# TensorE in program order through attention, with one unit behind each weight block, a scaled input in PSUM, and queries scaled before they are rotated

## The chip, the cores and the metric

The kernel runs on one core of a Trainium2 chip. The metric is the time of one execution on the device in microseconds (us), smaller is better; runs of one kernel on one chip lie within a few tenths of a per cent. The engines of the core work side by side, each in the order of its own instructions: TensorE (PE in the rows, PEld for its weight loads), VectorE (DVE), ScalarE (ACT), GpSimd (POOL), and SyncE (SP), which here only issues DMAs. SBUF and PSUM are the on-chip memories; TensorE writes into PSUM.

## What is computed

Two layers over T = 256 tokens of width D = 2048, with a context of 256 tokens that only layer 0 reads. Everything is fp32. Cut to what matters here:

```python
# layer 0
h  = rmsnorm(x, g0) * (1 + scale) + shift            # scale, shift, gate = silu(c) @ ada_w + ada_b
hc = rmsnorm(ctx, g0) * (1 + scale_c) + shift_c
k, v, q, za, glu, zb = split(h @ w_in)               # 2 KV heads, 8 query heads of 128
q  = rope(rmsnorm(q) * q_norm);  k = rope(rmsnorm(k) * k_norm)
kc, vc = split(hc @ w_in[:, :512])                   # context keys and values
s  = (q @ concat(k, kc).T) * 128 ** -0.5             # per head: 256 queries x 512 keys
attn = softmax(s) @ concat(v, vc)
conv = silu(layernorm(depthwise_conv31(a * sigmoid(b)) + dw_b))    # a, b = split(glu), 1024 channels
x  = x + gate * (concat(attn * silu(za), conv * silu(zb)) @ w_out0)
# layer 1: adaLN-RMSNorm, projection, spatial gating, output projection, gated residual; then a final RMSNorm
```

## The kernel before

**Products.** Each fp32 matrix is split into a high and a low part, and each product is three TensorE instructions: high by high, high by low, low by high (L386, L388, L389 for 128x256 outputs, L409 to L411 for the 128x512 outputs of the queries, L560 to L564 for keys and values). The weights come as jobs of 512 KB, one block each. A job has a load (a DMA on SP's queue into `raw`, a ring of ten buffers), a split (ACT copies `raw` to `whi`, L361; then DVE or GpSimd makes `wlo` = `raw` − `whi`, L364; GpSimd has the jobs 30 to 133), and its products. `whi` and `wlo` have four buffers each.

**Modulation jobs.** Between the weight jobs lie others ("A" jobs) that make the modulation of the gate of layer 0 and of layer 1. They load `traw` into the same ring, and DVE works on each in two instructions (L274, in PSUM operand `cbp`). They have no TensorE work.

**The scaled input.** `make_h` makes the operand h of layer 0 (`h0`, names `h` in the trace) and of the context (`hc`) four blocks of 128 columns at a time: DVE makes `ht` = x · scale · 1/rms (L453), ACT adds the shift and rounds to the high part (L456), DVE makes the low part from `ht` and the high part (L460). `ht` lies in SBUF.

**PSUM.** Eight banks of 128x512: three for `acc` (products, and every second score), one for the score `S`, one for the convolution, one for `cbp`, two for all else (tag "m").

**Attention.** Keys and queries are normalised per head (`head_rstd`, L720 to L724: squares `sqj` on ACT, a root, a reciprocal), rotated (`rope`, L709 to L714, queries on DVE, keys on GpSimd), and transposed on TensorE. For each of 16 pieces (key head, half of the queries, query head): a score (`attn_head`, L776), its maximum on DVE (L779, L780), exp on ACT (L782) with the query's norm as its scale, four transposes `ptp` of the result P (L796), and for each two pieces a product `O` with the values (L807). `AD` = 3 is the distance between a score and its transposes.

**Order.** The Python program lists the segments and the "side" work, attention and convolution steps, which it hands out behind weight jobs:

```python
for _ in range(math.ceil((PACEA if key == "attn" else PACE) * len(side[key]) / max(1, left))):
```

So the number of steps behind a weight job follows from the steps left and the jobs left (`PACEA` = 1.25). The final order of each engine is set by the scheduler of the language, which estimates when each instruction can start; inside a priority it moves instructions past each other. The segments of layer 0 are, in order: the conv's projections with keys and values (`body`); the first half of the queries (`qa`), four blocks of the gate `za`, and the second half (`qb`); the rest of `za`; the gate of the convolution; and the output projection.

Of the kernel before, what the change touches and what calls it, by code (L numbers as in the profile page):

```python
# [44 lines left out]
P2 = 4  # L45
# [40 lines left out]
def backbone_kernel(  # L86
# [146 lines left out]


# [135 lines left out]
    def w_rows(jobs, src, kbs, h, post):  # L370
# [3 lines left out]
        for n, (kq, kts) in enumerate(parts):  # L374
            def mmf(jb, kq=kq, n=n, kts=kts):
# [3 lines left out]
                for kt in kts:  # L379
                    hh, hl = h(kq * 4 + kt)  # L380
                    k = kt - kts[0]
                    for b in range(2):
# [3 lines left out]
                        nc.tensor.matmul(o, wh, hh, start=(n == 0 and kt == kts[0] and b == 0), stop=False,  # L386
                                         skip_group_check=True)
                        nc.tensor.matmul(o, wh, hl, start=False, stop=False, skip_group_check=True)  # L388
                        nc.tensor.matmul(o, wl, hh, start=False, stop=end, skip_group_check=True)  # L389
# [4 lines left out]
    def w_cols(jobs, src_f, kbs, hs, post):  # L394
# [3 lines left out]
        for n, (kp, kts) in enumerate(parts):  # L398
            def mmf(jb, kp=kp, n=n, kts=kts):
# [3 lines left out]
                for i, (h, ch) in enumerate(hs):  # L403
                    for k, kt in enumerate(kts):
# [4 lines left out]
                        nc.tensor.matmul(accs[i], hh[:, sl], jb.hi[:, k, :], start=s0, stop=False)  # L409
                        nc.tensor.matmul(accs[i], hh[:, sl], jb.lo[:, k, :], start=False, stop=False)  # L410
                        nc.tensor.matmul(accs[i], hl[:, sl], jb.hi[:, k, :], start=False, stop=s1)  # L411
# [130 lines left out]

    def kv_part(kqs):
# [3 lines left out]
        for cg in range(2):  # L547
            accs = {}
            for kq in kqs:
                def mmf(jb, cg=cg, kq=kq, accs=accs):  # L550
                    for i, h in enumerate((hx, hcx)):
                        if kq == kqs[0]:
                            accs[i] = bank("acc")
                        for k in range(4):
                            hh, hl = h(kq * 4 + k)
                            for c in range(2):
# [5 lines left out]
                                nc.tensor.matmul(o, hh[:, sl], jb.lo[:, k, :], start=False, stop=False,  # L562
                                                 skip_group_check=True)
# [140 lines left out]
    def rope(dst, src, nm, c, nh, eng, t1, t2):  # L704
# [487 lines left out]
```

## Time and profile before

| | |
|---|---|
| runs shown | median 926.71 us of 3 (925.51 to 928.1) |
| profiled execution | 926.46 us, span 924.7 us |
| granted TensorE clock, mean | 0.975 |
| busy: TensorE, DVE, ACT, POOL | 872.9, 659.6, 457.9, 258.6 us |
| DMA | 239.06 MB, mean 259 GB/s |

A row of the timeline has the start and the length in us, the engine, the line of the kernel, the operation, what is written and read (buffer numbers left out), shape and type, and a count; in brackets stands how long the engine was idle before it and whose end released it. A group's row has its busy time, the mean ns of one, and the idle time before its instructions. A stage's row has the stretch, its length, the busy time of each engine with the number of its instructions, the granted clock, the share of the DMA engines' time and the GB/s.

### The profile page before, as it was taken

To read this page: it belongs to the slowest core of one execution; us is meant where nothing else is said; L and a number is where in the kernel's file an instruction comes from. 1 tells how busy PE (TensorE), PEld (TensorE's weight loads), DVE (VectorE), ACT (ScalarE), POOL (GpSimd) and SP (SyncE) were. 2 spreads that over 40 slices of the span, in tenths; PEclk is the share of its full clock that TensorE was granted. 3 is DMA by queue.
4 is the path that set the end of the run, shared out by engine and by line. 5 is a ranking of instruction groups with operands and counts; after the bars stand their busy time and mean duration, and the time that the engine had idled before them with its cause. 6 is when DMAs were issued, how large, how long until landed. Compare 5 with 4: busy or idle time off the path is not lost.

```text
span 924.7 us, 17928 instructions
## 1 busy us (share of the span) xinstructions
PE 872.9 (94%) x7084; PEld 800.5 (87%) x7084; DVE 659.6 (71%) x1413; ACT 457.9 (50%) x648; POOL 258.6 (28%) x125
## 2 busy tenths in 40 slices
PE   5999999599998689999999899999999999999994
PEld 3798899599887578998999778998899999999994
DVE  2355684978887877895765299998988977554442
ACT  5643242347557668545544544455583544444441
POOL 0000023659875235686777520000000000000000
PEclk9999999799999899999999899999999999999998
DMA  9999999685776332678889579988887788755402
GB/s 355 406 389 352 363 338 365 252 286 173 233 247 217 121 114 91 205 249 298 312 311 342 175 277 410 409 312 304 311 281 225 250 282 281 218 185 174 137 1 91
DMA packets 66864, 239.06 MB, mean 259 GB/s; under 512 B 7502, under 2 KB 7768, under 8 KB 66268
## 3 DMA queue, kind: packets, MB, share of 16 engines
q1 hardware_dynamic: 66780, 237.92, 72.9%
q8 instruction: 55, 0.90, 0.4%
q14 instruction: 29, 0.24, 0.1%
HBM read 235.80 MB, written 2.10 MB: 257 GB/s over the span
## 4 chain that ended last, share of the span: by engine, by line
PE 76%; DVE 10%; DMA 10%; ACT 3%; issue 1%; POOL 0%; SPq 0%; DVEq 0%; POOLq 0%; ACTq 0%
PE acc L386 17%; PE acc L389 16%; PE acc L388 16%; DMA traw<-adat 7%; PE acc L409 4%; PE acc L410 4%; PE acc L411 4%; DVE traw L274 4%; PE ada L317 3%; PE acc L560 2%; PE acc L562 2%; PE acc L564 2%; DVE conv L626 1%; DMA braw<-ada 1%; PE rms L191 1%
## 5 line engine op out<-in xcount | busy, mean ns | idle before, releaser
L361 ACT ACTIVATE whi<-raw 128x1024 fp32r<-128x1024 f32 (+1 forms) x256 | 263.4, 1031 | 285.1 <-PE acc L388 140.4
L364 POOL TENSOR_TENSOR wlo<-raw,whi 128x1024 fp32r<-128x1024 f32 x104 | 250.9, 2425 | 283.3 <-ACT whi L361 145.4
L364 DVE TENSOR_TENSOR wlo<-raw,whi 128x1024 fp32r<-128x1024 f32 (+1 forms) x152 | 176.8, 1165 | 83.3 <-ACT whi L361 81.7
L274 DVE SCALAR_TENSOR_TENSOR traw<-traw,cbp 128x512 f32<-128x512 f32 x256 | 165.3, 682 | 56.0 <-DMA traw<-adat 52.7
L386 PE MATMUL acc<-h,whi 128*128 128x256 f32 x512 | 152.4, 299 | 8.0 <-DVE gaT L532 6.7
L388 PE MATMUL acc<-h,whi 128*128 128x256 f32 x512 | 149.3, 293 | 0.4 <-DVE h L460 0.4
L389 PE MATMUL acc<-h,wlo 128*128 128x256 f32 x512 | 148.0, 290 | 1.6 <-POOL wlo L364 1.6
L388 PE MATMUL acc<-h1l,whi 128*128 128x256 f32 x512 | 145.2, 284 | 0.0
L389 PE MATMUL acc<-h1h,wlo 128*128 128x256 f32 x512 | 145.0, 283 | 0.0
L386 PE MATMUL acc<-h1h,whi 128*128 128x256 f32 x512 | 145.0, 283 | 0.0
L626 DVE SCALAR_TENSOR_TENSOR conv<-gaT,small,conv 128x241 f32<-128x241 f32 (+14 forms) x240 | 114.6, 478 | 5.2
L386 PEld LDWEIGHTS acc<-h,whi 128*128 128x128 f32 x512 | 100.6, 197 | 14.1 <-issue 10.3
L389 PEld LDWEIGHTS acc<-h,wlo 128*128 128x128 f32 x512 | 100.5, 197 | 4.1 <-issue 2.0
L388 PEld LDWEIGHTS acc<-h,whi 128*128 128x128 f32 x512 | 100.7, 197 | 3.5 <-issue 2.6
L388 PEld LDWEIGHTS acc<-h1l,whi 128*128 128x128 f32 x512 | 98.2, 192 | 0.1
L386 PEld LDWEIGHTS acc<-h1h,whi 128*128 128x128 f32 x512 | 98.2, 192 | 0.1
L389 PEld LDWEIGHTS acc<-h1h,wlo 128*128 128x128 f32 x512 | 98.2, 192 | 0.0
L389 PE MATMUL acc<-m1h,wlo 128*128 128x256 f32 x256 | 73.1, 286 | 0.0
L386 PE MATMUL acc<-m1h,whi 128*128 128x256 f32 x256 | 72.4, 283 | 0.0
L388 PE MATMUL acc<-m1l,whi 128*128 128x256 f32 x256 | 72.4, 283 | 0.0
L389 PEld LDWEIGHTS acc<-m1h,wlo 128*128 128x128 f32 x256 | 49.1, 192 | 2.9 <-issue 2.9
L411 PE MATMUL acc<-whi,h1l 128*128 128x512 f32 x128 | 51.1, 400 | 0.0
(235 smaller groups left out, 1649.1 us busy)
## 6 DMA issues: line engine op xcount, KB each, us to landing
traw<-adat SPq DMA_DIRECT2D x128, 512.0 KB, 5.0
raw<-w_out SPq DMA_DIRECT2D x64, 512.0 KB, 4.0
raw<-w_uz SPq DMA_DIRECT2D x64, 512.0 KB, 4.9
araw<-ada SPq DMA_DIRECT2D x56, 512.0 KB, 6.9
raw<-w_gate SPq DMA_DIRECT2D x56, 512.0 KB, 5.1
raw<-w_v SPq DMA_DIRECT2D x32, 512.0 KB, 5.1
raw<-w_q SPq DMA_DIRECT2D x16, 512.0 KB, 4.1
raw<-w_gate SPq DMA_DIRECT2D x16, 256.0 KB, 11.0
```

The lines of the kernel that those rows point to most:

```text
L274: nc.vector.scalar_tensor_tensor(out=jb.raw[:, k, :], in0=jb.raw[:, k, :], scalar=1.0, in1=cbq["t"], op0=ALU.mult, op1=ALU.mult, accum_out ...
L317: nc.tensor.matmul(st8["p"][32 * g : 32 * g + 32, :w], ccol[:, kb, :], jb.raw[:, a, q * w : (q + 1) * w], start=kb < 4 // nq, stop=kb >= N ...
L361: nc.scalar.activation(hv, jb.raw, AF.Copy)
L364: eng.tensor_tensor(out=jb.lo.rearrange("p a b -> p (a b)"), in0=jb.raw, in1=hv.bitcast(F32), op=ALU.subtract)
L386: nc.tensor.matmul(o, wh, hh, start=(n == 0 and kt == kts[0] and b == 0), stop=False, skip_group_check=True)
L388: nc.tensor.matmul(o, wh, hl, start=False, stop=False, skip_group_check=True)
L389: nc.tensor.matmul(o, wl, hh, start=False, stop=end, skip_group_check=True)
L409: nc.tensor.matmul(accs[i], hh[:, sl], jb.hi[:, k, :], start=s0, stop=False)
L410: nc.tensor.matmul(accs[i], hh[:, sl], jb.lo[:, k, :], start=False, stop=False)
L411: nc.tensor.matmul(accs[i], hl[:, sl], jb.hi[:, k, :], start=False, stop=s1)
L560: nc.tensor.matmul(o, hh[:, sl], jb.hi[:, k, :], start=kq == kqs[0] and k == 0 and c == 0, stop=False, skip_group_check=True)
L626: nc.vector.scalar_tensor_tensor(out=o, in0=y, scalar=w, in1=o, op0=ALU.mult, op1=ALU.add)
```

## The change

Five things change.

1. TensorE's instructions are held in program order from the first half of the queries to the start of layer 1: each is issued after the one before it in the program. Before, the scheduler was free to move them.
2. One attention step is now one `unit`: a score, the transposes of the piece three units back, and, every second time, a product with the values. One stands behind each weight block. The turns (transposes) of keys and queries are steps of their own; behind the second half of the queries two blocks have no step (`rest`). Attention steps and the query's rope run at high priority.
3. In `make_h`, `ht` of layer 0 and the context lies in a PSUM bank (tag "m").
4. `rope` works in place on its input, with two temporaries in SBUF; for queries the input is the product's PSUM bank.
5. Queries are scaled by their norm before the rotation (four ACT instructions of 128x128 for each 128 tokens and half), so that the score needs no scale: the maximum is taken negated in one DVE instruction, and L780 is gone. `P2`, which had no effect (`nw % 4 < 4`), goes.

```diff
+    pe = {"on": False}
+    def inorder(op, *args, **kw):
+        with tc.issue_after(pe["last"]) if pe["on"] and "last" in pe else nullcontext():
+            i = op(*args, **kw)
+        pe["last"] = i.ins
+    def matmul(*args, **kw):
+        inorder(nc.tensor.matmul, *args, **kw)
...
-            t = tmp.tile([128, 2, T], F32, tag="t2", name="ht", bufs=TB)
+            if m == 4:
+                t = bank("ht").rearrange("p (a b) -> p a b", a=2)
+            else:
+                t = tmp.tile([128, 2, T], F32, tag="t2", name="ht", bufs=TB)
...
-    def rope(dst, src, nm, c, nh, eng, t1, t2):
+    def rope(dst, src, nm, c, nh, eng):
         e, o = src[:, :, 0:64], src[:, :, 64:128]
-        eng.tensor_tensor(out=t1, in0=e, in1=tb(0), op=ALU.mult)
+        eng.tensor_tensor(out=t1, in0=e, in1=tb(2), op=ALU.mult)
+        eng.tensor_tensor(out=e, in0=e, in1=tb(0), op=ALU.mult)
         eng.tensor_tensor(out=t2, in0=o, in1=tb(1), op=ALU.mult)
-        eng.tensor_tensor(out=dst[:, :, 0:64], in0=t1, in1=t2, op=ALU.subtract)
-        eng.tensor_tensor(out=t1, in0=e, in1=tb(2), op=ALU.mult)
-        eng.tensor_tensor(out=t2, in0=o, in1=tb(3), op=ALU.mult)
-        eng.tensor_tensor(out=dst[:, :, 64:128], in0=t1, in1=t2, op=ALU.add)
+        eng.tensor_tensor(out=o, in0=o, in1=tb(3), op=ALU.mult)
+        eng.tensor_tensor(out=dst[:, :, 0:64], in0=e, in1=t2, op=ALU.subtract)
+        eng.tensor_tensor(out=dst[:, :, 64:128], in0=o, in1=t1, op=ALU.add)
...
-        at["rq"][i, cg] = head_rstd(src, 4, "qss", HD ** -0.5)
+        r = head_rstd(src, 4, "qss", HD ** -0.5)
+        for h in range(4):
+            nc.scalar.activation(src[:, h * 128 : (h + 1) * 128], src[:, h * 128 : (h + 1) * 128], AF.Copy, scale=r[:, h : h + 1])
...
-        nc.vector.tensor_reduce(out=mx[:, 0:1], in_=S, axis=AX.X, op=ALU.max)
-        nc.vector.tensor_scalar(out=mx[:, 1:2], in0=mx[:, 0:1], scalar1=rq, scalar2=-1.0, op0=ALU.mult, op1=ALU.mult)
+        nc.vector.tensor_reduce(out=mx[:, 1:2], in_=S, axis=AX.X, op=ALU.max, negate=True)
-        nc.scalar.activation(P, S, AF.Exp, bias=mx[:, 1:2], scale=rq, accum_out=mx[:, 2:3])
+        nc.scalar.activation(P, S, AF.Exp, bias=mx[:, 1:2], accum_out=mx[:, 2:3])
...
+        def unit(n):
+            if n < len(todo):
+                attn_head(*todo[n])
+            if n > AD and (n - AD) % 2 == 0:
+                attn_pv(*todo[n - AD - 1])
+            if AD <= n < len(todo) + AD:
+                attn_tr(*todo[n - AD])
...
-    segs = [body, qa + kv[0] + za[:4] + qb, kv[1] + za[4:] + [za_ready], ...
+    segs = [body, [pe on] + qa + za[:2] + kv[0] + za[2:4] + qb + [rest = 2], za[4:8] + kv[1] + za[8:] + [za_ready], ...
```

The lines move by ten or more: L276 to L287 stand for L274 before, L377 for L364, L469 and L476 for L453 and L460, L548 for L532, L786 for L782; all wrapped TensorE instructions have L238. How the order of the instructions moves, at three places. The numbers behind the names are those of the buffers and differ between the two kernels.

The first place is DVE's order around the block of keys and values before the queries. `gaT` and `gbT` add up the products of `acc` and so free the banks that TensorE needs; `h0` and `hc` are the low parts of the input. Before:

```order
L532 TENSOR_TENSOR kv_sb_820<-acc_2139,kv_sb_820 128x2x256
L460 SCALAR_TENSOR_TENSOR h0_2267<-ht_2268,modv0_133,h0_2267 128x256
L274 SCALAR_TENSOR_TENSOR traw_2073,adat_139<-traw_2073,cbp_2219 128x512 x2
L460 SCALAR_TENSOR_TENSOR h0_2267<-ht_2268,modv0_133,h0_2267 128x256
L460 SCALAR_TENSOR_TENSOR h0_2267<-ht_2275,modv0_133,h0_2267 128x256 x2
L460 SCALAR_TENSOR_TENSOR hc_2491<-ht_2492,modc_135,hc_2491 128x256
L532 TENSOR_TENSOR gaT_136<-acc_2179,gaT_136 128x512
```

And after:

```order
L287 SCALAR_TENSOR_TENSOR traw_2063,adat_139<-traw_2063,cbp_2219 128x512
L548 TENSOR_TENSOR gaT_136<-acc_2179,gaT_136 128x512
L287 SCALAR_TENSOR_TENSOR traw_2063,adat_139<-traw_2063,cbp_2219 128x512
L476 SCALAR_TENSOR_TENSOR h0_2267<-ht_2268,modv0_133,h0_2267 128x256 x2
L476 SCALAR_TENSOR_TENSOR h0_2267<-ht_2275,modv0_133,h0_2267 128x256 x2
L287 SCALAR_TENSOR_TENSOR traw_2073,adat_139<-traw_2073,cbp_2219 128x512 x2
L287 SCALAR_TENSOR_TENSOR traw_2089,adat_139<-traw_2089,cbp_2219 128x512 x2
L469 SCALAR_TENSOR_TENSOR ht_2492<-cT1_325,modc_135,rBc_613 128x256
L548 TENSOR_TENSOR gbT_137<-acc_2225,gbT_137 128x512
```

`gaT` now stands ahead of all four `h0` of that group and of `hc`; the `ht` of the context comes later, and `gbT` behind its first.

The second place is TensorE's order in the score products (`S`, or `acc` for the score that takes a product's bank). Before, behind the second half of the queries, among the blocks of `za`:

```order
L776 MATMUL S_3411<-kT_2564,qT_3072 128x512
...
L776 MATMUL acc_3678<-kT_2564,qT_3072 128x512
L776 MATMUL S_3500<-kT_2564,qT_3072 128x512
L776 MATMUL S_3623<-kT_2564,qT_3072 128x512
L386 MATMUL acc_3801<-h0_316,whi_3644 128x256
```

And after, inside the second half of the queries:

```order
L238 MATMUL S_3358<-kT_2564,qT_3060 128x512
L238 MATMUL acc_3280<-whi_3276,h0_1090 128x512
...
L238 MATMUL S_3388<-kT_2564,qT_3060 128x512
L238 MATMUL acc_3280<-whi_3312,h0_1655 128x512
...
L238 MATMUL S_3423<-kT_2564,qT_3060 128x512
L238 MATMUL ptp_3432<-ident_86,P_3332 128x128 x4
```

Three scores in a row became one score behind the twelve products of each block; seven of the sixteen stand inside the second half of the queries, where two stood before.

The third place is what stands between these scores on DVE, and ahead of an exp on ACT. DVE after, between the maxima of two scores (`traw` is a modulation job, L633 the convolution):

```order
L784 TENSOR_REDUCE mx_3360<-S_3358 128x1
L633 SCALAR_TENSOR_TENSOR conv_2950<-gaT_136,small_84,conv_2950 128x250
L633 SCALAR_TENSOR_TENSOR conv_2950<-gaT_136,small_84,conv_2950 128x249
L287 SCALAR_TENSOR_TENSOR traw_3522,adat_140<-traw_3522,cbp_2991 128x512 x2
L787 RECIPROCAL mx_3360<-mx_3360 128x1
L633 SCALAR_TENSOR_TENSOR conv_2950<-gaT_136,small_84,conv_2950 128x248
L266 COPY cbp_3991<-cb_105 128x512
L784 TENSOR_REDUCE mx_3390<-S_3388 128x1
```

A pair of `traw` stands between two maxima, and its instruction needs the transfer of its job. ACT after, behind the second half of the queries (`whi` are splits of weight jobs, the scalings have `acc` in and out):

```order
L222 ACTIVATE qss_3565<-qss_3565,epsc_97 128x4
L766 ACTIVATE acc_3280<-acc_3280,qss_3540 128x128 x2
L374 ACTIVATE whi_3649<-raw_3409 128x1024
L766 ACTIVATE acc_3281<-acc_3281,qss_3565 128x128 x4
L374 ACTIVATE whi_3683<-raw_3478 128x1024
L374 ACTIVATE whi_3741<-raw_3608 128x1024
L786 ACT_TABLE_LOAD
L786 ACTIVATE P_3594,mx_3592<-S_3590,mx_3592 128x512
```

The exp of the last score of that half now stands behind the scalings and three splits.

More of the change, by code (lines that the diff above doesn't have):

```diff
@@ L44 @@
 L1 = 2
-P2 = 4
 NF = 3
@@ L385, in mmf @@
                         end = n == len(parts) - 1 and kt == kts[-1]
-                        nc.tensor.matmul(o, wh, hh, start=(n == 0 and kt == kts[0] and b == 0), stop=False,
+                        matmul(o, wh, hh, start=(n == 0 and kt == kts[0] and b == 0), stop=False,
                                          skip_group_check=True)
-                        nc.tensor.matmul(o, wh, hl, start=False, stop=False, skip_group_check=True)
-                        nc.tensor.matmul(o, wl, hh, start=False, stop=end, skip_group_check=True)
+                        matmul(o, wh, hl, start=False, stop=False, skip_group_check=True)
+                        matmul(o, wl, hh, start=False, stop=end, skip_group_check=True)
                 if n == len(parts) - 1:
@@ L582, in post @@
             def post(i, a, cg=cg):
-                rope_q(i, cg, a)
-                side["attn"].append(lambda: turn_q(i, cg))
+                with tc.high_priority():
+                    rope_q(i, cg, a)
             w_cols(js, lambda kp, cg=cg: w_q[cg, kp], range(16), [(hx, 0), (hx, 1)], post)
@@ L738, in rope_k @@
         if i < 2:
-            t1 = tmp.tile([128, 2, 64], F32, tag="rp1", name="rp1", bufs=1)
-            t2 = tmp.tile([128, 2, 64], F32, tag="rp2", name="rp2", bufs=1)
-            rope(kr, s3, "k", i, 2, nc.gpsimd, t1, t2)
+            rope(kr, s3, "k", i, 2, nc.gpsimd)
         else:
@@ L828, in attn_steps, with both @@
     def attn_steps():
-        out, half = [], 0
+        def both(f, *args):
+            return lambda: [f(i, *args) for i in range(2)]
+        out = [both(turn_k), lambda: [turn_k(i) for i in (2, 3)], both(turn_q, 0)]
         todo = [(kvh, c, hq) for kvh in range(NKV) for c in range(2) for hq in range(4)]
-        for n in range(len(todo) + AD):
-            if n == len(todo) // 2:
-                half = len(out)
-            if n < len(todo):
-                out.append(lambda n=n: attn_head(*todo[n]))
-            if n >= AD:
-                out.append(lambda n=n: attn_tr(*todo[n - AD]))
-                if (n - AD) % 2 == 1:
-                    out.append(lambda n=n: attn_pv(*todo[n - AD]))
-        out.append(("za", attn_gate))
-        out += [lambda: attn_fin(0), lambda: attn_fin(1)]
-        return out[:half], out[half:]
+        def unit(n):
[5 more added lines that the diff above has]
+                attn_tr(*todo[n - AD])
+        for n in range(len(todo) + AD + 1):
+            if n == len(todo) // 2:
+                out.append(("q", both(turn_q, 1)))
+            out.append(lambda n=n: unit(n))
+        return out + [("za", attn_gate), lambda: attn_fin(0), lambda: attn_fin(1)]
     def hm(kb):
@@ L1024, in drain @@
             s = side[key].pop(0)
-            (s[1] if isinstance(s, tuple) else s)()
+            with tc.high_priority() if key == "attn" else nullcontext():
+                (s[1] if isinstance(s, tuple) else s)()
             k += 1
@@ L1065, in backbone_kernel @@
     ada1b = adat_pair(1, 1024, D + 1024)
-    plan += [hook(lambda: prep1(0)), hook(sgu_const)]
+    plan += [hook(lambda: pe.__setitem__("on", False)), hook(lambda: prep1(0)), hook(sgu_const)]
     first = v_part(0) + u_part(0)
@@ L1074, in backbone_kernel @@
         if j.kind == "W":
-            j.pool = P0 <= nw < P1 and nw % 4 < P2
+            j.pool = P0 <= nw < P1
             nw += 1
@@ L1107, in backbone_kernel @@
             for key in ("attn", "conv"):
+                if key == "attn" and st.get("rest"):
+                    st["rest"] -= 1
+                    continue
                 ahead = [n for k, n in deadline.items() if k == key and n > p]
@@ L1110, in backbone_kernel @@
                 for _ in range(math.ceil((PACEA if key == "attn" else PACE) * len(side[key]) / max(1, left))):
-                    if side[key] and isinstance(side[key][0], tuple) and side[key][0][0] == "za" and "za" not in st:
+                    if side[key] and isinstance(side[key][0], tuple) and side[key][0][0] not in st:
                         break
```

48 lines of the change are left out of this document (20 added, 28 removed).

## The prediction

> **What bounds the kernel now.** I read the page first, then a table of the span by stage, then the waits of TensorE (PE) in the stretch that the change touches, and last the rows around the longest waits.
>
> ```profile
> span 924.7 us, 17928 instructions
> PE 872.9 (94%) x7084; PEld 800.5 (87%) x7084; DVE 659.6 (71%) x1413; ACT 457.9 (50%) x648; POOL 258.6 (28%) x125
> PE 76%; DVE 10%; DMA 10%; ACT 3%; issue 1%; POOL 0%; SPq 0%; DVEq 0%; POOLq 0%; ACTq 0%
> ```
>
> TensorE is busy 94% of the span and carries 76% of the chain that ended last. The change takes no product away, so it can only win time in which TensorE stands still or runs at a low clock: 924.7 − 872.9 = 51.8 us of idle time at most. The table by stage (stretch, its length, then busy time of PE, weight load, DVE, ACT, POOL with counts, granted clock, DMA share, GB/s) shows where it lies.
>
> ```profile
> 100.00:150.00 50.00, 50.00 (x626) 45.55 (x628) 31.43 (x59) 13.88 (x20) 8.29 (x3) 1.00 0.93 345
> 150.00:183.00 33.00, 23.65 (x212) 22.51 (x200) 29.33 (x54) 11.77 (x18) 19.55 (x8) 0.89 0.83 323
> 183.00:252.00 69.00, 68.81 (x466) 64.94 (x467) 55.95 (x135) 38.53 (x79) 52.43 (x34) 0.96 0.69 225
> 252.00:300.00 48.00, 45.43 (x251) 37.95 (x250) 39.49 (x103) 31.67 (x54) 32.57 (x14) 0.96 0.68 231
> 300.00:340.00 40.00, 30.35 (x166) 23.24 (x164) 31.91 (x83) 24.49 (x36) 14.62 (x7) 0.87 0.39 125
> 340.00:380.00 40.00, 40.00 (x286) 36.51 (x285) 34.49 (x90) 29.36 (x48) 18.09 (x8) 1.00 0.36 112
> 430.00:480.00 50.00, 49.45 (x405) 47.54 (x404) 34.38 (x92) 27.17 (x37) 38.24 (x16) 1.00 0.86 309
> ```
>
> Two stretches have room: 150 to 183 (9.4 us idle) and 252 to 340 (2.6 + 9.7 = 12.3 us idle, at a clock of 0.87 in the second half). From 340 on TensorE is full. In both the change moves something.
>
> **The first stretch, and what scaled input in PSUM does to it.** These rows stand around the idle time before 183 us.
>
> ```profile
> 156.30 2.39 POOL L364 TENSOR_TENSOR wlo<-raw,whi 128x1024 fp32r<-128x1024 f32 x1 [1.83 <-PE acc L562]
> 157.16 0.69 DVE L532 TENSOR_TENSOR kv_sb<-acc,kv_sb 128x512 f32<-128x512 f32 x1
> 161.40 2.40 POOL L364 TENSOR_TENSOR wlo<-raw,whi 128x1024 fp32r<-128x1024 f32 x1 [2.71 <-ACT whi L361]
> 161.45 2.38 DVE L344 SCALAR_TENSOR_TENSOR modc<-modc,small 128x4 f32<-128x4 f32 x1
> 164.97 1.66 DVE L453 SCALAR_TENSOR_TENSOR ht<-xT,modv,rB 128x256 f32<-128x256 f32 x4
> 169.81 12.35 POOL L364 TENSOR_TENSOR wlo<-raw,whi 128x1024 fp32r<-128x1024 f32 x5 [6.00 <-ACT whi L361]
> 172.22 0.58 PE L389 MATMUL acc<-h,wlo 128*128 128x256 f32 x1 [1.57 <-POOL wlo L364]
> 173.59 6.38 DVE L460 SCALAR_TENSOR_TENSOR h<-ht,modv,h 128x256 fp32r<-128x256 f32 x3
> 179.89 2.56 DVE L460 SCALAR_TENSOR_TENSOR hc<-ht,modc,hc 128x256 fp32r<-128x256 f32 x1
> 182.37 0.68 DVE L532 TENSOR_TENSOR gaT<-acc,gaT 128x512 f32<-128x512 f32 x1
> 183.19 0.55 PE L386 MATMUL acc<-h,whi 128*128 128x256 f32 x1 [6.68 <-DVE gaT L532]
> 184.18 1.27 DVE L460 SCALAR_TENSOR_TENSOR hc<-ht,modc,hc 128x256 fp32r<-128x256 f32 x3
> ```
>
> While GpSimd runs `wlo`, a DVE instruction with two SBUF tensors as input takes as long as the `wlo` that it meets: `modc` needs 2.38 us for 4 columns, `h` 6.38 us for three and `hc` 2.56 us for one, where three `hc` take 1.27 us with GpSimd idle. An instruction with one input in PSUM isn't held: `kv_sb` took 0.69 us in the middle of a `wlo`. In the order of DVE, `gaT` stands behind the held instructions, and it frees the bank that TensorE needs: 6.68 us.
>
> The change puts `ht` into PSUM. `h` and `hc` (L476 now) then have one SBUF input, so their four held instructions fall from 6.38 + 2.56 = 8.9 us to 4 x 0.42 = 1.7. The instruction that makes `ht` (L469) still reads two SBUF tensors, `xT` and `rB`. In the trace none of them met a `wlo` (1.66 us for four), so its price when it does is bounded by 0.42 us and, from `modc`, 2.4 us; I take 2.4 for each that meets one. I walked the new order with these durations. ACT now does `whi_2007` after the first two `h0`, so GpSimd's `wlo` before the gap starts at 164.9 instead of 161.4; TensorE waits for it 1.3 us longer at about 166. `wlo_2110` starts at 169.8 as before, TensorE goes on at 172.2 as before, and has 24 products of that block ahead, which at the pitch of the slow clock end at about 176.8. It then needs `gbT` of the block before, which stands behind one `ht`; that meets `wlo_2208` until 177.0, ends at 177.5, and `gbT` ends at 178.2. So TensorE goes on at about 178.3 instead of 183.19: a gain of 4.9 us; the 1.3 us are in it, since they only shorten the later wait. If no `ht` is held it goes on at 176.8, a gain of 6.4; if five more `ht` are held (5 x 2.4 us), the stretch gets 7 us longer. I take −5, between −6.4 and +7.
>
> The Trainium skill, SBUF — State Buffer, section "SBUF: two separate sides", says that DVE and GpSimd take a shared port pair as an exclusive lock for a whole instruction, a DVE instruction with two SBUF inputs among them. By that rule each `ht` that meets a `wlo` is held to its end, which no row here shows for `ht`; the rows of `h`, `hc`, `modc` and `kv_sb` (2.5, 2.56, 2.38 and 0.69 us) agree with it.
>
> **The second stretch: attention.** TensorE's waits there, and the rows that end them:
>
> ```profile
> 290.29 2.24 PE L807 MATMUL O<-PT,kv_sb 128*128 128x256 f32 x7 [2.57 <-ACT PT L797]
> 303.27 1.13 PE L776 MATMUL S<-kT,qT 128*128 128x512 f32 x2 [1.67 <-ACT P L782]
> 308.45 2.03 PE L776 MATMUL acc<-kT,qT 128*128 128x512 f32 x2 [2.99 <-ACT z0T L601]
> 314.65 1.41 PE L776 MATMUL S<-kT,qT 128*128 128x512 f32 x2 [2.25 <-ACT P L782]
> 335.29 1.57 PE L776 MATMUL S<-kT,qT 128*128 128x512 f32 x2 [2.59 <-ACT qT L770]
> ```
>
> They sum to 12.1 us. They come of bunching: score products `S` stand two and three in a row, and the second waits for max and exp of the first, since the bank `S` is one. The change lays one unit (one S, the transposes of an older P, every second time a P·V) behind each weight block, in fixed order, so 12 products of a block lie between two `S`. What one unit costs, by rows:
>
> ```profile
> 258.21 0.39 PE L411 MATMUL acc<-whi,h 128*128 128x512 f32 x1
> 258.44 0.40 PE L409 MATMUL acc<-whi,h 128*128 128x512 f32 x1
> L779 DVE TENSOR_REDUCE mx<-S 128x1 f32<-128x512 f32 x11 | 7.5, 686 | 4.0 <-PE S L776 3.9
> 313.72 0.78 ACT L782 ACTIVATE P<-S,mx,qss 128x512 f32<-128x512 f32 x1 [1.45 <-DVE mx L780]
> L780 DVE TENSOR_SCALAR mx<-mx,qss 128x1 f32<-128x1 f32 x16 | 3.1, 204 | 0.0
> 306.51 1.28 ACT L601 ACT_TABLE_LOAD   x1
> 283.80 1.04 ACT L361 ACTIVATE whi<-raw 128x1024 fp32r<-128x1024 f32 x1
> 284.75 0.26 ACT L720 ACTIVATE sqj<-acc 128x128 f32<-128x128 f32 x1
> 262.10 4.43 DMA traw<-adat
> 268.31 4.41 DMA traw<-adat
> 274.57 4.52 DMA traw<-adat
> 279.18 0.69 DVE L274 SCALAR_TENSOR_TENSOR traw<-traw,cbp 128x512 f32<-128x512 f32 x1 [1.06 <-DMA traw<-adat]
> ```
>
> Twelve products at 0.23 us are 2.75 us between two `S`. Max (0.69) and exp (0.78) take 1.5 us, so a unit passes without a wait if its max isn't late. What makes it late is the modulation work of layer 1 on DVE, pairs of `traw` instructions (2 x 0.69), each pair behind a transfer that lands 4.4 us after the pair before it has freed its buffer. Four such pairs stand between the units of the second half of the queries, each ahead of a max. So a pair comes every 6.2 us (262.10, 268.31, 274.57), and a unit lasts 2.75 + 0.9 for S + 0.4 for transposes, some 4 us. The pairs that matter end, by the walk, at 265.2, 271.0, 276.8 and 282.6; behind each come one to three small conv instructions (0.42 each), a max and an exp, so that the bank `S` is free at 268.8, 274.0, 279.7 and 284.2. TensorE would want it at 269.2, 272.8, 277.6 and 283.7 (each is the start of the `S` before, with its wait, plus the unit): the first unit has slack, and the next three wait 1.2, 2.1 and 0.5 us.
>
> The other new waits, each from the order: at the start of the second query half TensorE needs a bank that `z0T` reads, which stands in ACT behind a `whi` (1.04) and a table load (1.28): 1.04 + 1.28 + 0.6 less 1.4 us of products and 0.4 of transposes, 1.2 us. Behind the last block of that half, exp of `P_3594` stands in ACT behind eight `sqj` (0.26 and more each), the root with its table load, eight scalings, four `whi` and another table load. The last of these `whi` waits for a product that ends 0.2 us before TensorE wants the next `S`, so TensorE waits 1.04 + 1.28 + 0.78 = 3.1 us. In all 1.2 + 3.8 + 3.1 = 8.1 us of new waits against 12.1 that go: −4.0. The slower clock behind a wait costs both sides; 40 us at 0.87 with 30.35 busy is at most 0.13 x 30.35 = 3.9 us before, and two thirds of that for two thirds of the waits, −1.3. Sum for attention −5; its ends are −12 (all new waits vanish) and +8 (next part).
>
> **Edits at nothing.** The 16 scalings of the queries are new on ACT; the row nearest is `sqj`, 0.26 us, so 4.2 us, all in the two stretches behind a query half, where I counted them. The 16 `mx` instructions of L780 that go (3.1 us on DVE) are 0.2 us per unit on a chain that has slack. Rope in place has the same six operations with an input in PSUM; its bank is held some 1 us longer, and TensorE gets there later than that. Dropping P2 changes no job. Between 340 and 380 the DMA share is 0.36, so an earlier start of the output projection can load ahead; between 430 and 480 it is 0.86 at 309 GB/s, and since every transfer waits for a buffer that TensorE's progress frees, the whole plan shifts with TensorE.
>
> **The sum.** −5 −5 = −10. The profiled execution took 926.46 us (span 924.7), the median of the runs is 926.71, so 0.25 apart; I predict 916.6. A change under 0.3% (2.8 us) can't be told from none in this kernel.
>
> **Rivals.**
> Both stretches win (forecast), 912 to 921: chance 0.45.
> Only the first wins: the waits in attention are replaced in kind, −5, 921.5 to 923. For it: the new waits are as long as the old ones, and the order is held, so nothing fills them. Chance 0.18.
> All attention waits go, since a `traw` lands sooner when the rings run ahead: −5 −12 = 909 to 911. For it: in 252 to 300 the DMA share is only 0.68. Against: the pairs come 6.2 us apart in that very stretch. Chance 0.15.
> Slower: the transfers of `traw` set the pace of the units. If the max of each of the seven units in that half stands behind a pair, a unit takes 6.2 instead of 4 us: 7 x 2.2 = 15.4 new, and 4.3 for the two others, against 12.1 that go, +7.6, and nothing from the first stretch: 934; with the first stretch's gain 929. It decides from the point where more than five of the seven wait so. Against it: the order has four pairs there, not seven. Chance 0.12.
> No change: the `ht` instructions are held in place of `h` and `hc`, so that the first stretch wins nothing, and attention trades like for like: 924 to 928. Five more held `ht` at 2.4 us undo the first gain and what attention wins. Chance 0.10. The rule of the Trainium skill named above (SBUF — State Buffer, "SBUF: two separate sides") would have it so wherever an `ht` meets a `wlo`.
>
> The likeliest range is 912 to 921; so that the other cases are in, 907 to 927. Faster: 0.45 + 0.18 + 0.15 = 0.78; same 0.10; slower 0.12.
>
> **What would show it.** First stretch right: no `h` or `hc` of L476 over 0.6 us before 190 us, and the wait for `gaT` or `gbT` under 3 us; wrong: `ht` of L469 with 2.4 us each. Attention right: `S` strictly one per block, waits of 0.5 to 2.1 us put down to P, with a `traw` ahead of the max, and one of about 3 us behind the second query half; the waits for z0T and for two S in a row gone. The prediction is wrong if the waits in the units are over 2.5 us each, if the block matmuls wait for a rope (bank held), or if TensorE idles after 400 us where it didn't.

## The result, and the profile after

The changed kernel takes 916.9 us (median, 914.78 to 919.12, 4 runs), the kernel before 927.4 on the same chip: a ratio of 0.9884, 95% interval 0.9857 to 0.9911. The forecast was 916.6, of 907 to 927. The sum is right; of its parts, the one for attention is too small, and a loss behind attention was missed, as shown below. Profiled executions of kernels that hardly differ up to 210 us end keys and values anywhere between 200.9 and 206.4 us (table below), so a difference of a few microseconds between two single profiles shows nothing alone.

The page of the profile after: the span, each engine's busy time, and the chain that ended last.

```profile
span 913.0 us, 17916 instructions
PE 867.9 (95%) x7084; PEld 799.7 (88%) x7084; DVE 649.8 (71%) x1397; ACT 457.6 (50%) x662; POOL 257.5 (28%) x125
PE 79%; DMA 9%; DVE 7%; ACT 2%; issue 1%; POOL 1%; SPq 0%; DVEq 0%; POOLq 0%; ACTq 0%
```

DVE's share of the chain fell from 10 to 7%. By stage (columns as in the prediction):

```profile
150.00:183.00 33.00, 29.43 (x282) 27.76 (x274) 26.76 (x64) 13.18 (x20) 18.32 (x8) 1.00 0.98 389
252.00:300.00 48.00, 42.55 (x218) 33.41 (x218) 41.64 (x114) 36.79 (x75) 29.74 (x13) 1.00 0.66 212
300.00:340.00 40.00, 39.46 (x263) 34.42 (x264) 34.62 (x82) 28.55 (x46) 18.00 (x8) 0.96 0.44 139
430.00:480.00 50.00, 47.82 (x380) 46.33 (x379) 36.35 (x93) 24.10 (x31) 36.41 (x16) 0.97 0.90 324
```

The stretch 150 to 183 is busy for 29.4 us instead of 23.7, and 300 to 340 for 39.5 instead of 30.4, at a clock of 0.96 instead of 0.87. From 430 to 480, TensorE idles 2.2 us where it idled 0.6. These stretches are cut by time, and the work in them has moved.

Three rows of TensorE's timeline in each kernel cut the span at the same work: the last product of keys and values, the first of the output projection (`mAh`), and the first of layer 1. Before, then after:

```profile
211.64 0.28 PE L564 MATMUL acc<-whi,hc 128*128 128x256 f32 x1
416.62 0.28 PE L386 MATMUL acc<-mAh,whi 128*128 128x256 f32 x1
529.33 0.80 PE L409 MATMUL acc<-whi,h1h 128*128 128x512 f32 x1
```

```profile
205.85 0.28 PE L238 MATMUL acc<-whi,hc 128*128 128x256 f32 x1
401.40 0.28 PE L238 MATMUL acc<-mAh,whi 128*128 128x256 f32 x1
516.02 0.80 PE L238 MATMUL acc<-whi,h1h 128*128 128x512 f32 x1
```

The gain is 5.8 us at the end of keys and values, 15.2 at the output projection, 13.3 at layer 1, and 11.7 in the span. So in this pair of profiles the first stretch gave 5.8, attention 9.4, and 3.5 were given back after it. The stages between these cuts hold the same products (attention, output projection, layer 1; before, then after; a count that differs by one is a record missing from a trace):

```profile
211.92:416.62 204.70, 192.48 (x1241) 170.08 (x1240) 174.29 (x432) 126.66 (x205) 130.00 (x65) 0.97 0.57 186
416.62:529.33 112.71, 107.26 (x861) 99.10 (x859) 62.02 (x164) 55.34 (x73) 79.66 (x34) 0.99 0.82 289
529.33:924.70 395.37, 383.51 (x2805) 361.04 (x2804) 294.76 (x533) 190.02 (x227) 4.77 (x2) 0.98 0.70 244
```

```profile
206.13:401.40 195.27, 187.56 (x1241) 167.22 (x1240) 167.58 (x410) 126.78 (x216) 130.60 (x67) 0.99 0.62 196
401.40:516.02 114.62, 109.44 (x860) 101.11 (x859) 64.40 (x169) 55.09 (x73) 79.78 (x34) 0.97 0.82 285
516.02:913.00 396.98, 385.37 (x2805) 362.32 (x2804) 295.35 (x533) 190.05 (x227) 4.77 (x2) 0.98 0.71 242
```

Attention's 9.4 us are 4.5 us less idle time of TensorE (7.7 instead of 12.2) and 4.9 us less busy time for the same products, at a clock of 0.99 instead of 0.97. The same cuts for every kernel that ran, from its profiled execution, with the timed ratio to the kernel before (95% interval):

| kernel | keys/values end | to first mAh | to layer 1 | ratio |
|---|---|---|---|---|
| before | 211.9 | 204.7 | 112.7 | 1 |
| changed | 206.1 | 195.3 | 114.6 | 0.9884 (0.9857 to 0.9911) |
| e1 changed, ht in SBUF | 213.4 | 196.8 | 117.1 | 0.9956 (0.9932 to 0.9981) |
| e2 before, ht in PSUM | 203.4 | 200.7 | 114.7 | 0.9900 (0.9867 to 0.9933) |
| e3 changed, no hold | 204.3 | 191.8 | 115.3 | 0.9811 (0.9764 to 0.9858) |
| e4 before, hold | 211.6 | 217.9 | 114.5 | 1.0144 (1.0096 to 1.0191) |
| e5 changed, norm in the exp | 204.4 | 196.4 | 120.3 | 0.9841 (0.9795 to 0.9886) |
| e6 changed, PACE 2.0 | 204.6 | 196.6 | 115.2 | 0.9855 (0.9801 to 0.9910) |
| e7 changed, modulation earlier | 200.9 | 195.4 | 134.2 | 1.0016 (0.9988 to 1.0044) |
| e8 changed, no rest | 204.3 | 200.6 | 114.5 | 0.9851 (0.9816 to 0.9886) |
| e9 before, splits of GpSimd from job 40 | 207.5 | 204.0 | 113.9 | 0.9934 (0.9910 to 0.9958) |
| e10 no hold, splits from job 40 | 203.8 | 192.5 | 112.4 | 0.9786 (0.9757 to 0.9815) |
| e11 no hold, norm in the exp | 204.9 | 193.5 | 118.5 | 0.9823 (0.9801 to 0.9844) |
| e12 no hold, PACE 2.0 | 206.4 | 194.6 | 112.1 | 0.9798 (0.9765 to 0.9831) |

The runs were made in several rounds, each beside the kernel before, whose median moved between 926.6 and 929.9 us. So kernels of different rounds are compared by their ratios rather than by their microseconds.

### The profile page after: what moved, and what is told of

The parts are those of the page before. It is cut to its first block, busy times and chain, and to the rows that moved or that the text cites. A ratio compares the mean times of both kernels' runs of the same rounds, so it can differ in the third digit from the quotient of the medians.

```text
span 913.0 us, 17916 instructions
## 1 busy us (share of the span) xinstructions
PE 867.9 (95%) x7084; PEld 799.7 (88%) x7084; DVE 649.8 (71%) x1397; ACT 457.6 (50%) x662; POOL 257.5 (28%) x125
## 4 chain that ended last, share of the span: by engine, by line
PE 79%; DMA 9%; DVE 7%; ACT 2%; issue 1%; POOL 1%; SPq 0%; DVEq 0%; POOLq 0%; ACTq 0%
PE acc L238 69%; DMA traw<-adat 7%; DVE traw L287 3%; PE ada L330 3%; PE O L238 2%; PE rms L190 1%; DVE ht L469 1%; DMA araw<-ada 1%; PE S L238 1%; PE sgu L962 1%; PE ptp L238 1%; POOL wlo L377 1%; DMA cin<-ccol 1%; ACT whi L374 1%; DVE conv L633 1%
## 5 line engine op out<-in xcount | busy, mean ns | idle before, releaser
L377 POOL TENSOR_TENSOR wlo<-raw,whi 128x1024 fp32r<-128x1024 f32 x104 | 250.0, 2414 | 273.4 <-ACT whi L374 272.9
L377 DVE TENSOR_TENSOR wlo<-raw,whi 128x1024 fp32r<-128x1024 f32 (+1 forms) x152 | 176.6, 1164 | 91.2 <-ACT whi L374 89.5
L238 PE MATMUL acc<-h,whi 128*128 128x256 f32 x1024 | 194.1, 290 | 5.4 <-DVE gaT L548 2.8
L287 DVE SCALAR_TENSOR_TENSOR traw<-traw,cbp 128x512 f32<-128x512 f32 x256 | 165.1, 681 | 47.6 <-DMA traw<-adat 46.4
L238 PEld LDWEIGHTS acc<-h,whi 128*128 128x128 f32 x1024 | 162.4, 195 | 10.4 <-ACT whi L374 4.1
L238 PE MATMUL acc<-h,wlo 128*128 128x256 f32 x512 | 145.8, 286 | 1.7 <-POOL wlo L377 1.7
L238 PE MATMUL acc<-h1l,whi 128*128 128x256 f32 x512 | 145.2, 284 | 0.0
L238 PE MATMUL acc<-h1h,wlo 128*128 128x256 f32 x512 | 145.0, 283 | 0.0
L238 PE MATMUL acc<-h1h,whi 128*128 128x256 f32 x512 | 145.0, 283 | 0.0
L633 DVE SCALAR_TENSOR_TENSOR conv<-gaT,small,conv 128x241 f32<-128x241 f32 (+14 forms) x240 | 114.6, 477 | 5.2
L238 PEld LDWEIGHTS acc<-h,wlo 128*128 128x128 f32 x512 | 99.4, 194 | 2.1 <-POOL wlo L377 2.1
L238 PEld LDWEIGHTS acc<-h1h,whi 128*128 128x128 f32 x512 | 98.2, 192 | 0.1
L238 PEld LDWEIGHTS acc<-h1l,whi 128*128 128x128 f32 x512 | 98.2, 192 | 0.1
L238 PEld LDWEIGHTS acc<-h1h,wlo 128*128 128x128 f32 x512 | 98.2, 192 | 0.0
L238 PE MATMUL acc<-m1h,wlo 128*128 128x256 f32 x256 | 73.1, 286 | 0.0
L238 PE MATMUL acc<-m1h,whi 128*128 128x256 f32 x256 | 72.4, 283 | 0.0
L238 PE MATMUL acc<-m1l,whi 128*128 128x256 f32 x256 | 72.4, 283 | 0.0
L238 PE MATMUL acc<-whi,h 128*128 128x256 f32 (+1 forms) x256 | 68.0, 346 | 1.3 <-ACT z0T L608 1.3
L238 PEld LDWEIGHTS acc<-whi,h 128*128 128x128 f32 x256 | 44.6, 189 | 8.2 <-ACT z0T L608 1.7
L238 PEld LDWEIGHTS acc<-m1h,wlo 128*128 128x128 f32 x256 | 49.1, 192 | 2.9 <-issue 2.9
L238 PE MATMUL acc<-whi,h1l 128*128 128x512 f32 x128 | 51.2, 402 | 0.0
```

The costliest lines, as they stand in the source:

```text
L238: i = op(*args, **kw)
L287: nc.vector.scalar_tensor_tensor(out=jb.raw[:, k, :], in0=jb.raw[:, k, :], scalar=1.0, in1=cbq["t"], op0=ALU.mult, op1=ALU.mult, accum_out ...
L377: eng.tensor_tensor(out=jb.lo.rearrange("p a b -> p (a b)"), in0=jb.raw, in1=hv.bitcast(F32), op=ALU.subtract)
L633: nc.vector.scalar_tensor_tensor(out=o, in0=y, scalar=w, in1=o, op0=ALU.mult, op1=ALU.add)
```

## Experiments: the first stretch

**e1, ht back in SBUF.**

```diff
-            if m == 4:
+            if False:
                 t = bank("ht").rearrange("p (a b) -> p a b", a=2)
```

> The changed kernel with ht back in SBUF (change 3 undone), all else as changed. Theory A (held instructions): four h and hc meet a wlo of GpSimd again and last 1.4 to 2.6 us each; the wait for gaT before 185 us is 6 us or more again, the last product of keys and values ends near 212 us as before (206.1 in the changed kernel), and the time is 5 to 6 us over the changed kernel (916.9), 921.5 to 923. Rival B (the new order of DVE alone made the gain there): the last product ends at 206 to 207 us and the time stays within 2 us of 916.9. Rival C (the later conv chain limits the output projection anyway): lost early, but made up by 460 us, within 2 us of 916.9 though the early part is slow.

Measured: 922.8 us, ratio 0.9956. Groups of DVE between 30 and 190 us, and TensorE's longest wait:

```profile
L476 DVE SCALAR_TENSOR_TENSOR h<-ht,modv,h 128x256 fp32r<-128x256 f32 x14 | 15.4, 1138 | 0.0
L476 DVE SCALAR_TENSOR_TENSOR hc<-ht,modc,hc 128x256 fp32r<-128x256 f32 x16 | 11.0, 740 | 0.0
PE acc L238 <- DVE gaT L548: 8.1, 1, 8.1
```

`h` is back at 1138 ns on average, as in the kernel before, and the wait for `gaT` at 8.1 us. The ends of keys and values and the time are those of theory A; B and C fall.

**e2, ht in PSUM alone.** The kernel before with the same three lines of `make_h`.

> The kernel before with ht in PSUM and nothing else (change 3 alone). Theory A: no h or hc of layer 0 is over 0.6 us, the wait of 6.7 us for gaT falls under 3 us, the last product of keys and values ends at 206 to 207 us (211.9 before), and the time is 4 to 6 us under before: 921 to 923. Rival B (order, not the bank): under 2 us of gain, 925 or more.

Measured: 919.4 us, ratio 0.9900, which can't be told from the whole change's 0.9884: the intervals overlap. Keys and values end at 203.4. Theory A, with a gain over what it said (7.2 us by the medians, 9.3 by the ratio). `ht` is in SBUF with the same splits on GpSimd in three profiles (before, e1, e4), which end keys and values at 211.6 to 213.4 us; it is in PSUM in nine, which end at 200.9 to 206.4. That the first stretch gains is clear; its size, between the middle ones, is 7.5 us, and 5.8 lies at the low end.

**e9, the kernel before, with fewer splits on GpSimd.**

```diff
-P0 = 30
+P0 = 40
```

> The kernel before, with ht in SBUF as it was, but GpSimd makes wlo only from weight job 40 on (30 before): the ten splits between 131 and 182 us, the ones that the held instructions met, are DVE's now. Theory A (an instruction with two SBUF inputs is held by a GpSimd instruction that runs): no h or hc of layer 0 lasts over 0.6 us though ht is in SBUF; DVE gains 8 us and pays 10 x 1.2 us for the splits; the wait of 6.7 us for gaT falls under 4 us, and the last product of keys and values ends at 205 to 210 us (211.9 before). Rival B (it is ht in SBUF that makes them slow): they last 1.4 to 2.6 us as before, and it ends at 212 us or later.

Measured: 923.0 us, ratio 0.9934. The groups of DVE between 30 and 190 us, `ht` being in SBUF:

```profile
L460 DVE SCALAR_TENSOR_TENSOR hc<-ht,modc,hc 128x256 fp32r<-128x256 f32 x16 | 6.8, 484 | 0.0
L460 DVE SCALAR_TENSOR_TENSOR h<-ht,modv,h 128x256 fp32r<-128x256 f32 x14 | 6.1, 482 | 0.0
```

482 ns instead of 1138 with the same operands: `ht` in SBUF alone doesn't make them long; it takes a GpSimd instruction that runs beside them. Theory A. The gain is 0.7% where e2's was 1.0% (the intervals overlap). DVE now makes ten splits, and TensorE waits 3.7 us for `gbT` instead of 6.7 for `gaT`.

## Experiments: attention

**e3, no hold.**

```diff
-    segs = [body, [hook(lambda: pe.__setitem__("on", True))] + qa + za[:2] + ...
+    segs = [body, qa + za[:2] + ...
```

> The changed kernel with TensorE not held in program order (change 1 undone), units and all else kept. Theory A (spacing by the program, kept by the hold): the scheduler moves scores and transposes again, two or three scores stand in a row or far behind their block, and waits of 1.5 to 3 us come back: 5 to 10 us over the changed kernel, 922 to 927. Rival B (the units alone space the scores, the hold is idle): within 2 us of 916.9. Rival C (the hold costs, since TensorE cannot pass a blocked score): 2 to 5 us faster, 912 to 915.

Measured: 910.4 us, ratio 0.9811: rival C, by more than it said. TensorE's waits between 150 and 530 us, in the changed kernel first (total, times, longest), then without the hold:

```profile
PE S L238 <- ACT P L786: 4.3, 3, 3.2
PE acc L238 <- DVE gaT L548: 2.8, 1, 2.8
PE acc L238 <- DVE mBl L454: 1.7, 1, 1.7
PE acc L238 <- POOL wlo L377: 1.7, 2, 1.3
PE acc L238 <- ACT z0T L608: 1.3, 1, 1.3
PE O L238 <- ACT PT L801: 1.1, 1, 1.1
PE ktp L238 <- ACT kT L758: 1.0, 1, 1.0
```

```profile
PE S L238 <- ACT P L786: 4.3, 1, 4.3
PE cmean L190 <- ACT gaT L636: 3.5, 1, 3.5
PE acc L238 <- DVE gaT L548: 2.8, 1, 2.8
```

Without the hold the waits for z0T, PT and kT are gone (3.4 us): the scheduler is free to lay other products there. From keys and values to `mAh` it is 191.8 instead of 195.3, 3.4 us less, with TensorE busy for 187.6 us in both: the whole difference is idle time. The waits that the units meant to avoid don't come back. So the units space the scores, and the hold costs. Two more pairs say the same (e5 against e11, e6 against e12): by the ratios the hold costs 6.8, 1.7 and 5.3 us. All have one sign, but in no pair do the intervals lie wholly apart (those of e3 and the changed kernel meet at 0.9857). The size stays open between some 2 and 7 us.

**e4, the hold alone.** The kernel before, with the wrappers of the change around the same instructions.

> The kernel before with TensorE held in program order through attention and nothing else (change 1 alone; steps as before). Theory A (hold and units only work together): the steps are handed out in bursts behind the blocks, so scores and what hangs on them follow each other, waits add up: slower than before, 928 to 940. Rival B (the hold alone brings the attention gain): 917 to 921.

Measured: 941.4 us, ratio 1.0144: theory A, and a little beyond its upper end of 940. Two of TensorE's rows:

```profile
250.67 1.08 PE L239 MATMUL qtp<-ident,qr 128*128 128x128 f32 x4 [5.04 <-DVE qr L728]
310.32 1.09 PE L239 MATMUL ptp<-ident,P 128*128 128x128 f32 x4 [10.01 <-DVE qr L728]
```

Transposes stand in TensorE's order ahead of what they need, and what follows cannot pass. The second waits for the query's rope, though it transposes P: by the code, the old rope's temporary `rp` lies in the same two banks (tag "m") as `ptp`. That this is the reason is read from the code and the releaser, not tried alone.

**e5, the norm back in the exp.**

```diff
+        at["rq"][i, cg] = head_rstd(src, 4, "qss", HD ** -0.5)
...
+        nc.vector.tensor_scalar(out=mx[:, 1:2], in0=mx[:, 0:1], scalar1=rq, scalar2=-1.0, op0=ALU.mult, op1=ALU.mult)
-        nc.scalar.activation(P, S, AF.Exp, bias=mx[:, 1:2], accum_out=mx[:, 2:3])
+        nc.scalar.activation(P, S, AF.Exp, bias=mx[:, 1:2], scale=rq, accum_out=mx[:, 2:3])
```

> The changed kernel with the queries' norm back in the exp (change 5 undone: no scaling on ACT, L780 back on DVE), hold, units and rope in place kept. Theory A (the eight scalings behind the second query half delay the exp that TensorE waits 3.2 us for): this wait falls under 1.5 us and the time by 1 to 3 us, 914 to 916. Rival B (that exp waits behind a weight split that itself waits for TensorE, whatever stands before it): the wait stays over 2.5 us and the time within 1.5 us of 916.9. Rival C (the scaling saves DVE time on each unit's chain): 1 to 3 us slower, 918 to 920.

Measured: 915.9 us, ratio 0.9841. The longest wait for P is 4.5 us; it did not fall with the scalings, so theory A's mechanism is out, and the wait is rival B's. The time lies in the ranges of both; by the ratio it is 4 us under the changed kernel, with overlapping intervals.

**e11, the same without the hold.**

> The changed kernel without the hold and with the queries' norm back in the exp: units, ht in PSUM and rope in place are left of the change. Theory A (the units give the attention gain, the scaling ahead is worth nothing, as with the hold: 915.9 against 916.9): within 2 us of 910.4. Rival B (scaling first also saves the exp's and max's chain): 3 us or more slower, 913 to 917.

Measured: 912.7 us, ratio 0.9823, over e3 by 2.3 us in the medians and by 1.1 in the ratios, and inside its interval: nearer to A, with B not shut out. Scaling ahead of the rotation is worth nothing that these runs can tell.

**e8, no blocks of rest.**

```diff
-... + qb + [hook(lambda: st.__setitem__("rest", 2))], za[4:8] ...
+... + qb, za[4:8] ...
```

> The changed kernel with no two blocks of rest behind the second query half. Theory A (the score there waits for an exp that stands behind a weight split of the third block): without the rest TensorE reaches the score two blocks, 5.8 us, earlier, and held in order waits for the scalings and roots instead: the wait grows from 3.2 to 5 us or more, 1 to 4 us slower, 918 to 921. Rival B (the split it waits for moves ahead with it): the wait is 3 us or less and the time within 1.5 us of 916.9.

Measured: 917.2 us, ratio 0.9851. In the profile the longest wait for P grew from 3.2 to 7.7 us and attention to 200.6, as theory A has it; the timed runs show no loss against the changed kernel, whose interval theirs overlaps. Its mechanism is seen, its price is not: inconclusive.

## Experiments: what is given back, and a faster version

**e6, faster convolution steps** (`PACE = 2.0` for 1.4).

> The changed kernel with the convolution's steps handed out faster (PACE 2.0 for 1.4). Of the 15 us that the first product of the output projection is early, 4 are gone at its end. Theory A (the convolution's chain on DVE and ACT ends too late for the earlier projection): its steps come earlier, the wait of 1.7 us for mBl and the one for mBh go, and the time falls by 1.5 to 4 us, 913 to 915.5. Rival B (the chain is bound by DVE's modulation work and its transfers, not by when its steps are handed out): the waits stay, within 1.5 us of 916.9.

Measured: 915.0 us, ratio 0.9855. The waits for mBl (1.6 us) and mBh (1.2) stay, and the one ahead of the convolution's mean grew from 0.3 to 1.6 us: rival B in the waits. The time lies in theory A's range, 2.7 us under the changed kernel by the ratio, but the intervals overlap: no difference is shown.

**e7, modulation jobs moved earlier.**

```diff
-EX = (4, 4, 8, 4, 14, 18)
+EX = (4, 4, 8, 10, 14, 12)
```

> The changed kernel with six modulation jobs moved from the second half of the output projection to the gate of the convolution (EX 10, 14, 12 at the end for 4, 14, 18), where the DMA share is 0.44 to 0.48. Theory A (traw instructions that wait for their transfer stand in DVE ahead of mBl): fewer of them after 430 us, the wait for mBl falls from 1.7 us to under 0.5, 1 to 3 us faster, 914 to 916. Rival B (they delay the convolution on DVE instead): mBl comes later, the wait grows, 1 to 4 us slower, 918 to 921.

Measured: 930.8 us, ratio 1.0016, far beyond rival B's number. The waits of TensorE that grew:

```profile
PE acc L238 <- ACT mBh L453: 7.3, 3, 3.6
PE cmean L190 <- ACT gaT L636: 4.7, 1, 4.7
PE acc L238 <- DVE mBl L454: 3.0, 2, 2.0
```

Six jobs more on DVE ahead of the convolution's end, and the output projection lasts 134.2 instead of 114.6 us, with 17.9 us of TensorE's idle time instead of 5.2 and a clock of 0.90 instead of 0.97. So the convolution's chain on DVE and ACT is what the output projection runs into, and modulation work in front of it is dear.

**e12, faster convolution steps without the hold.**

> The changed kernel without the hold, with PACE 2.0 for the convolution. Theory A (the wait of 3.5 us for the end of the convolution on ACT, which stands ahead of its mean on TensorE, comes of its steps being handed out late): it falls under 1.5 us and the time by 1 to 3 us, 907.5 to 909.5. Rival B (DVE's queue is full, steps handed out earlier only delay the units): the wait stays or moves into attention, 910 to 914.

Measured: 910.9 us, ratio 0.9798: the wait ahead of the mean fell from 3.5 to 1.7 us, that for P grew from 4.3 to 5.5 (two waits): rival B. By the ratio the time is 1.2 us under e3, inside its interval.

**e10, no hold, and GpSimd's splits from job 40.** The edits of e3 and e9 together.

> The changed kernel without the hold of TensorE's order (e3: 910.4 us), and GpSimd's splits from job 40 on. Theory A (the remaining wait of 2.8 us for gaT comes of ht of the context, held by wlo, as its two inputs are in SBUF): no ht is over 0.6 us, that wait goes, the last product of keys and values ends by 202 us (204.3 in e3): 907 to 909. Rival B (DVE pays more for ten splits than it wins): 911 to 914.

Measured: 908.2 us, ratio 0.9786, theory A in the time: the fastest of all, 2% under the kernel before. The wait for `gaT` is 0.3 us, but TensorE now waits 3.0 us for DVE's own `wlo` and 2.2 for `gbT`, and keys and values end at 203.8, as in e3: theory A's place of the gain isn't shown (one `ht` of the context still took 1.4 us). The time lies within e3's interval.

## Why the prediction was right, point by point

**The first stretch (−5 said, −5.8 in the profile).** The main step held: `h` and `hc` are free. DVE after, around the block that waited 6.7 us:

```profile
169.36 1.65 DVE L476 SCALAR_TENSOR_TENSOR h<-ht,modv,h 128x256 fp32r<-128x256 f32 x4
173.36 1.67 DVE L469 SCALAR_TENSOR_TENSOR ht<-cT,modc,rBc 128x256 f32<-128x256 f32 x1
175.54 4.96 DVE L469 SCALAR_TENSOR_TENSOR ht<-cT,modc,rBc 128x256 f32<-128x256 f32 x3
180.65 1.66 DVE L476 SCALAR_TENSOR_TENSOR hc<-ht,modc,hc 128x256 fp32r<-128x256 f32 x4
184.27 0.77 PE L238 MATMUL acc<-h,whi 128*128 128x256 f32 x2 [2.75 <-DVE gaT L548]
```

`h` and `hc` are at 0.42 us each; `ht`, with two inputs in SBUF, is now held in their place, 1.67 us for one and 4.96 for three, and `gaT` behind it costs TensorE 2.75 us instead of 6.68. The walk had the wait at `gbT` (here 0.4 us) rather than at the next `gaT`; the 1.3 us for `wlo` came as said. The walk had one `ht` held; between 30 and 190 us the sixteen of the context take 13.7 us instead of 6.7 (DVE's busy time), while `h` and `hc` together fall from 24.2 to 13.2. So more than half of what was saved was paid again, and the rival "no change" had the right mechanism. That −5 came so near is in part luck, since the walk missed both the number of held `ht` and the operand that TensorE waited for. The Trainium skill, SBUF — State Buffer, section "SBUF: two separate sides", has a DVE instruction with two SBUF inputs and a GpSimd one lock each other out; the trace agrees for `ht` (median 484 ns, longest 2624 in the row below) and e9 for `h` (482 ns without GpSimd's splits).

```profile
L469 DVE SCALAR_TENSOR_TENSOR ht<-cT,modc,rBc x16: 478/484/2624, 56.5 to 180.0; 128x256 f32<-128x256 f32 x16
```

That row has the shortest, median and longest `ht` of the context in ns.

**Attention (−5 said, −9.4 in the profile): the term that was mis-sized.** The new waits are nearly those of the list: z0T 1.3 us (1.2 said, though its terms add up to 1.1), the exp behind the second query half 3.2 (3.1), and in the units two of 0.45 and 0.65, where I had 1.2, 2.1 and 0.5. Two of 1.0 and 1.1 us (kT, PT) weren't foreseen. In all 7.7, of 8.1 said. ACT's rows show the 3.2 us as they were worked out, a late split, a table load, the exp:

```profile
297.34 1.06 ACT L374 ACTIVATE whi<-raw 128x1024 fp32r<-128x1024 f32 x1 [0.96 <-POOL wlo L377]
298.42 1.28 ACT L786 ACT_TABLE_LOAD   x1
299.71 0.69 ACT L786 ACTIVATE P<-S,mx 128x512 f32<-128x512 f32 x1
300.54 2.07 PE L238 MATMUL S<-kT,qT 128*128 128x512 f32 x2 [3.17 <-ACT P L786]
```

What made the split late was GpSimd's `wlo`, though, and not TensorE's products. The units' waits were smaller since the transfers of `traw` took 3.5 us and not 4.4 in two of four, so that pairs came 4.8 to 6.0 us apart. From the chain that ended last:

```profile
260.21 3.45 DMA traw<-adat
265.01 3.58 DMA traw<-adat
269.94 4.63 DMA traw<-adat
```

What failed is the clock's term. I let the new waits pay for slow clock like the old, and put the difference at −1.3. The rows of the stages say otherwise: the same products of attention kept TensorE busy for 187.6 us instead of 192.5, 4.9 us less, at 0.99 instead of 0.97, and the idle time fell by 4.5; together these are the 9.4. In this pair, the many short waits cost less clock than the few long ones did.

How much of it holds beyond this pair is less clear. Attention as it was took 200.7 to 204.7 us in three profiles (before, e2, e9), attention as changed, with the hold and the rest, 195.3 to 196.8 in five (changed, e1, e5, e6, e7). In the timed runs, everything but `ht` in PSUM gives 4.1 us alone (e1) and, on top of `ht` in PSUM, 1.5 us by the ratios or 3.3 by the medians, each against its own kernel before (e2 and the changed kernel, with overlapping intervals).

**Edits at nothing.** Right for the scalings (e5, e11). Wrong for the output projection: "the whole plan shifts with TensorE" is not so. Idle time after 400 us was named as a sign of being wrong, and a wait of 1.7 us for mBl and one of 0.5 for mBh are new there. Other waits went, so TensorE's idle time is 5.2 us against 5.5; the 1.9 us are in its busy time, 109.4 instead of 107.3. DVE's rows show why mBl is late, and the last row shows the clock behind the two waits:

```profile
452.79 0.69 DVE L287 SCALAR_TENSOR_TENSOR traw<-traw,cbp 128x512 f32<-128x512 f32 x1 [1.22 <-DMA traw<-adat]
458.94 0.68 DVE L287 SCALAR_TENSOR_TENSOR traw<-traw,cbp 128x512 f32<-128x512 f32 x1
459.55 0.69 DVE L454 TENSOR_TENSOR mBl<-cfin,mBh 128x512 fp32r<-128x512 f32 x1
460.29 0.38 PE L238 MATMUL acc<-mBl,whi 128*128 128x256 f32 x1 [1.71 <-DVE mBl L454]
460.00:465.00 5.00, 4.71 (x27) 4.71 (x27) 3.31 (x9) 1.69 (x2) 3.61 (x2) 0.66 1.01 364
```

The convolution's last parts come on DVE behind modulation work that waits for its transfers. That chain moved by 13 us where TensorE had moved by 16.7. Five us at 0.66 are 1.7 us by a rough count, near the 1.9. The loss stays small beside what single profiles differ by: e3 has no wait for mBl, though one of 3.5 us ahead of the convolution's mean, and its output projection takes 115.3 us. The other 1.6 us lie in layer 1, where they are no loss that can be told from chance: layer 1 takes between 394.2 and 397.6 us in all fourteen profiles.

**The sum** came out, in this pair of profiles, because an attention term 4.4 us too small met a loss of 3.5 that was missed: that is luck. The timed runs split the gain in another way than five and five: `ht` in PSUM gives 6.7 us (e1 against the changed kernel) to 9.3 (e2), all else 1.5 to 4.1. Of the rivals, "all attention waits go" was too high, and the slower one didn't come: the four pairs of `traw` gated two units, not five.

**The change's own idea.** Its first item, the hold, is a loss with the units (1.7 to 6.8 us) and a larger one without (13 us in attention, e4). What won is `ht` in PSUM (e1, e2) and, without the hold, the units (e2 to e11, 7 us, with the in-place rope, the high priority and the new order of the segments, which no run took apart).

## What to carry to other kernels

When a DVE instruction is several times longer than its twins, look at what GpSimd runs at that moment, and at whether both inputs lie in SBUF; one input in PSUM, or the GpSimd work elsewhere, frees it, but look at which instruction with two SBUF inputs meets GpSimd next. Time the parts of a change alone: here one of five gave most of it (0.9900, where all five give 0.9884). Space dependent work in the order that the program hands out, and hold TensorE in program order only where a run shows that it wins: here the spacing won and the hold lost. When a stage gets faster, ask which chain on another engine has to keep up with it next, and how far that chain moved.

## What was not expected of the hardware

With 5.5 us of idle time in 48 us (252 to 300, after), in waits of 0.45 to 1.3 us and the start of one of 3.2, the granted clock stayed at 1.00; with 9.7 in 40 us (300 to 340, before), in waits of 1.7 to 3.0, it was 0.87. That short waits are cheap in general is not shown: behind the 3.2 us the clock was 0.72 from 300 to 306 us, and behind two waits of 0.5 and 1.7 it was 0.66 from 460 to 465.

```profile
300.00:306.00 6.00, 5.46 (x21) 3.97 (x22) 5.76 (x16) 3.56 (x8) 1.18 (x1) 0.72 0.62 222
```

And an instruction with one input moved out passed part of its wait on to the next one with two SBUF inputs: no `ht` of the context took over 0.49 us before; after, the longest took 2.6.
